# Expert outputs rounded and scattered in float32r, and three half chunks per expert left unsplit

## The chip, the cores and the metric

One core of one Trainium2 chip. The metric is the device time of the whole program in microseconds (us); the kernel before takes 2283.22 us, the median of three runs (2280.13 to 2283.72).

## The reference

256 tokens of width 2048, all in float32. A conformer block (causal convolution, feed-forward) is followed by a second block, whose last part is a hierarchical mixture of 16 experts; the change lies there. Each token goes to 2 of 16 experts; an expert is `silu(x @ w_gate) * (x @ w_up)` of width 512, times the token's gate, times `w_down` back to 2048, and the outputs are summed into the tokens:

```python
hid = silu(einsum('td,edf->tef', t, w_gate)) * einsum('td,edf->tef', t, w_up)
y = einsum('tef,efd->td', hid * gate[:, :, None], w_down)
```

The result passes through a final RMS norm.

## The kernel before

**The weight stream.** All large weights come through one class, `Stream`. Its order is a list of chunks of 128 x 2048 float32 (1 MB). `load` issues one DMA per chunk from SP's queue into one of four `raw` buffers. A chunk is used as two halves of 128 x 1024. Each half is split for exactness: `hi` is the half rounded to float32r (a copy on ScalarE, line 74), `lo` is the rest (a subtraction on VectorE, line 83). In the expert stage `hi` is issued up to four halves ahead of the half being multiplied and `lo` up to three (`MOE_HI`, `MOE_LO`); there are 5 `hi` and 4 `lo` buffers. When the second half's `lo` has been issued, the chunk's buffer is given to the load four chunks later. TensorE multiplies the other operand, itself kept as a high and a low part, with `hi` and with `lo` (`product`: two matmuls of 512 columns, both float32r).

**The expert stage.** An expert has 16 half chunks of gate and up weights and 8 of down weights. The order of the turns is in(0), in(1), out(0), in(2), out(1), in(3), and so on to in(14), out(13), out(14), in(15), out(15); "in" is `into`, "out" is `down`. An expert holds 64 token slots. `into(e)` makes four matmuls per half; its 128 output rows are the 64 slots' high parts and low parts. `between(e)` then copies the two result banks out (line 1163 scales gate by the token's norm), folds the two row halves with float32 matmuls, applies silu, multiplies, and splits the hidden layer into high and low. These seven steps are run one per half during the next out. `down(e)` makes four matmuls per half; each two halves complete 512 output columns in one bank, and ScalarE copies the bank to `Yt` (line 1203). There are three `Yt` buffers.

**Scatter.** `scatter(k, es)` multiplies a 128 x 128 piece of `Yt` with the float32 matrix `sc` of the expert (slot to token, holding gate and norm), 256 columns in float32, for a pair of experts (e-1, e) with e even, into a spare bank; VectorE then adds the bank to the tokens `h` (line 1148). The scatters wait in a list `todo` and are filled in behind the products by a credit: each half adds 0.5 (0.1 where the next group's tokens are gathered, 0.3 in the last in), and a scatter of two experts costs 0.86.

**Order.** Each engine runs its instructions in the order in which the program issues them. One `beat` per half issues: `hi` and `lo` of later halves, then what was posted at the half before (copies out of banks, adds), then one step of `between`; then come the products and the fill. Gathers of the next four experts' tokens are done in in(0) and during in(3), in(7) and in(11), two 512-column copies' worth of work on ScalarE and TensorE per half.

**Before the expert stage** the same `Stream` feeds three matmuls of 256 or 272 columns per weight block, from about 17 us to about 1650 us of the span. `y` is a constant buffer of 16 KB per partition.

Of the kernel before, what the change touches and what calls it, by code (L numbers as in the profile page):

```python
# [7 lines left out]
F32 = mybir.dt.float32  # L8
# [4 lines left out]
OP = mybir.AluOpType  # L13
# [24 lines left out]
    VOFF[_name] = NV  # L38
    NV += _n

RAW_BUFS, HI_BUFS, LO_BUFS = 4, 5, 4
FILL_GU, FILL_DOWN, FILL_GATHER = 0.5, 0.5, 0.1
FILL_LAST = 0.3
LEAD, TURN, LATE, ON_PE = 3, 15, 4, 27
# [4 lines left out]
class Stream:  # L49
# [3 lines left out]
    def __init__(self, nc, raw, parts, order):  # L53
        self.nc, self.raw, self.parts, self.order = nc, raw, parts, order
        self.ahead, self.limit = (HI_BUFS, LO_BUFS), 2 * len(order)
        self.loaded = self.n_high = self.n_low = self.pos = 0
        self.raws, self.highs, self.lows = {}, {}, {}

    def load(self, upto):
        while self.loaded < min(upto, len(self.order)):  # L60
            t = self.raw.tile([P, 2048], F32, tag="raw", name=f"raw{self.loaded}")
            self.nc.sync.dma_start(out=t, in_=self.order[self.loaded][0])
            self.raws[self.loaded] = t
            self.loaded += 1

    def source(self, half):
        i, s = divmod(half, 2)
        self.load(i + 1)
        return self.raws[i][:, s * 1024 : (s + 1) * 1024]

    def high_to(self, halves):
        while self.n_high < halves:
            hi = self.parts.tile([P, 1024], F32R, tag="hi", bufs=HI_BUFS, name=f"hi{self.n_high}")
            self.nc.scalar.copy(hi, self.source(self.n_high))  # L74
            self.highs[self.n_high] = hi
            self.n_high += 1

    def low_to(self, halves):
        while self.n_low < halves:
            i, s = divmod(self.n_low, 2)  # L80
            eng = self.nc.gpsimd if self.order[i][1] else self.nc.vector
            lo = self.parts.tile([P, 1024], F32R, tag="lo", bufs=LO_BUFS, name=f"lo{self.n_low}")
            eng.tensor_tensor(lo, self.source(self.n_low), self.highs[self.n_low].bitcast(F32), OP.subtract)  # L83
            self.lows[self.n_low] = lo
            self.n_low += 1
            if s == 1:
                del self.raws[i]
                self.load(i + 1 + RAW_BUFS)

    def split_to(self, half, back=0):  # L90
        self.high_to(min(half + self.ahead[0] - back, self.limit))
# [40 lines left out]
def network(ctx, tc, a, out):  # L132
# [62 lines left out]
    y = const.tile([P, KB, T], F32, name="y")  # L195
# [751 lines left out]
    for k in range(14, KB):  # L947
        router(k)
    rn3 = small([2], "rn3")
    lt = wE.tile([20, T], F32, name="lt")  # L950
    natural_sums(pr, 2, lone)
    nc.scalar.copy(lt, lp)
    nc.scalar.activation(rn3, pr[:, 0:4:2], ACT.Sqrt, bias=eps6)
# [119 lines left out]
        nc.vector.tensor_reduce(nmore, more, AX, OP.add)  # L1073
        nc.vector.tensor_copy(nmore_i, nmore)

    yx = wE.tile([P, 8, T], F32, name="yx")
    Yt = [t.rearrange("p a t -> p (a t)") for t in (y[:, :8, :], y[:, 8:, :], yx)]

    def experts(hot, stream, extra):
        scat, rsl, hids, left = {}, {}, {}, [0] * NE  # L1080


        jobs, todo, posts, credit, ring = deque(), deque(), deque(), [0.0], deque((6, 7))
# [42 lines left out]
        def spread(e):  # L1126

            b, o = spare()
            for n in range(2):
                mm(o[:, n * T : (n + 1) * T], idt[: 2 * NE, n * NE + e : n * NE + e + 1].to_broadcast([2 * NE, P]), placeT, n == 0, True)  # L1130
            sc = wF.tile([P, T], F32, tag="sc", bufs=5, name=f"sc{e}_{turn_of[0]}")
            rs = wF.tile([P, 1], F32, tag="rs", name=f"rs{e}_{turn_of[0]}")

            def scale():
                nc.vector.scalar_tensor_tensor(sc, o[:, :T], slot_col, rb, OP.is_equal, OP.mult, accum_out=rs)
                nc.vector.tensor_tensor(sc, o[:, T:], sc, OP.mult)

            post(scale, b)
            scat[e], rsl[e] = sc, rs

        def scatter(k, es):
            b, o = spare()
            for n, e in enumerate(es):
                mm(o[:, :T], Yt[e % 3][:, k * P : (k + 1) * P], scat[e], n == 0, n == len(es) - 1)
                left[e] -= 1

            def add():
                nc.vector.tensor_tensor(h[:, k, :], h[:, k, :], o[:, :T], OP.add)
                if NE - 1 in es:
                    post(square)  # L1150

            def square():
                sq = square_to(k)
                nc.scalar.activation(sq, h[:, k, :], ACT.Square)
                post(lambda: add_square(sq, k, True))

            post(add, b)

        def between(e):
            gu = wF.tile([P, 2, 512], F32, tag="gu", bufs=1, name=f"gu{e}_{turn_of[0]}")  # L1160

            def out_of_bank():
                nc.scalar.activation(gu[:, 0, :], bank[0], ACT.Copy, scale=rsl[e])
                nc.scalar.copy(gu[:, 1, :], bank[1])

            def folded(g):

                for f in range(4):
                    mm(bank[4 + g][:, f * P : (f + 1) * P], gu[:, g, f * P : (f + 1) * P], fold, f == 0, True)

            view = lambda g: bank[4 + g].rearrange("p (f s) -> p f s", f=4)[:, :, :CAP]
            sg = wF.tile([P, 4, CAP], F32, tag="sg", bufs=1, name=f"sg{e}_{turn_of[0]}")
            hd = wF.tile([P, 4, P], F32R, tag="hd", name=f"hd{e}_{turn_of[0]}")
            hids[e] = hd

            def silu():
                nc.scalar.activation(sg, view(0), ACT.Silu)

            def high():
                nc.scalar.copy(hd[:, :, :CAP], sg)  # L1180
                if e == NE - 1:
                    nc.scalar.preload_act_table(ACT.Sqrt)

            return deque([out_of_bank, lambda: folded(0), lambda: folded(1),
                    silu,
                    lambda: nc.vector.tensor_tensor(sg, view(1), sg, OP.mult),
                    high,
                    lambda: nc.vector.tensor_tensor(hd[:, :, CAP:], sg, hd[:, :, :CAP].bitcast(F32), OP.subtract)])

        def down(e):  # L1190
            while e >= 3 and left[e - 3] > 0:
                todo.popleft()[1]()
            hd = hids.pop(e)
            left[e] = KB
            for c in range(4):
                o = bank[2 + c % 2]
                for n in range(2):
                    hi, lo = beat()
                    for f in range(2):
                        product(o, hd[:, 2 * n + f, :], hi, lo, f, n == 0 and f == 0, n == 1 and f == 1)  # L1200
                    if n == 1:
                        def out_of_bank(c=c, o=o):
                            nc.scalar.copy(Yt[e % 3][:, c * 512 : (c + 1) * 512], o)

                            es = (e,) if e in (0, NE - 1) else (e - 1, e)
                            if e == NE - 1 or e % 2 == 0:
                                for k in range(4 * c, 4 * c + 4):
                                    todo.append((0.43 * len(es), lambda k=k: scatter(k, es)))
                        post(out_of_bank)
                    fill(FILL_DOWN if e < NE - 1 else 1)  # L1210

        def into(e):
            nxt = one_hot(e // 4 + 1) if e % 4 == 3 and e + 1 < NE else None
            for k in range(KB):
# [6 lines left out]
                for kk in ([k - 3] if e == 0 else [k]) if k < KB - 1 or e else range(KB - 4, KB):  # L1221
# [3 lines left out]
                    w = X(kk)[:, (e % 4) * P : (e % 4 + 1) * P]  # L1225
                    for g in range(2):
                        product(bank[g], w, hi, lo, g, kk == 0, kk == KB - 1)
                    if extra is not None:
                        next(extra, None)
                    if kk == 13:  # L1230
# [28 lines left out]
                posts.popleft()()  # L1259


        natural_sums(bank[2], 2, lone)
        rsqrt(rp, bank[2][:, :4:2], eps6)
        to_all(rp, bank[3][:, :T])
        for k in range(KB):
            nc.vector.scalar_tensor_tensor(y[:, k, :], h[:, k, :], V("final", k), bank[3][:, :T], OP.mult, OP.mult)  # L1266
            if k in (1, 3, 7, 11, 15):
                k0 = {1: 0, 3: 2}.get(k, k - 3)
                nc.sync.dma_start(out=out[:, k0 : k + 1, :], in_=y[:, k0 : k + 1, :])

    experts(hot, stream, gates())
    turn_of[0] = "more"
# [65 lines left out]
```

## Time and profile before

| | |
|---|---|
| median of 3 runs | 2283.22 us (2280.13 to 2283.72) |
| the profiled execution | 2283.07 us, of which the span is 2281.3 us |
| TensorE (PE) busy | 2219.8 us, 97% |
| VectorE (DVE) busy | 1596.8 us, 70% |
| ScalarE (ACT) busy | 1255.5 us, 55% |
| DMA loads of weights | 460 of 1 MB each |
| expert stage, first product to start of the last out | 1679.6 to 2243.9 us |

PE's busy time is modelled: matmuls overlap, so the distance between two starts is the cost of one, not its duration. In the rows, `hi`, `lo`, `raw`, `sc`, `hd`, `gu`, `y`/`yx` (the buffers of `Yt`) and `x` (the tokens `h`) are the program's tiles. A float32 matmul stands in two records.

### The profile page before, as it was taken

The page shows a single profiled execution, that of the slowest core. Times are in us where ns is not written, and L with a number is a line of the kernel's source. Part 1 is how long each engine was busy: PE and PEld are TensorE (multiplying, and loading weights), DVE is VectorE, ACT ScalarE, POOL GpSimd, SP SyncE. Part 2 cuts the span into 40 slices and gives each one's busy share as a digit, 9 for nine tenths or more (in the row PEclk, how much of TensorE's full clock was granted, in tenths as well). Part 3 has the DMA queues.
Part 4 walks back from the last instruction along what each step waited for, and adds up shares of the span by engine and source line. Part 5 has one row for each costly group of instructions (what it writes and reads, how often), then busy time and mean ns, then how long its engine had stood idle before and what let it go on. Part 6 is the DMA issues. An engine that isn't in the chain of part 4 may idle for free. (4 is left out here: it accounts for less than half of the span.)

```text
span 2281.3 us, 40365 instructions
## 1 busy us (share of the span) xinstructions
PE 2219.8 (97%) x16539; PEld 2079.1 (91%) x16539; DVE 1596.8 (70%) x2259; ACT 1255.5 (55%) x1638; POOL 214.6 (9%) x162
## 2 busy tenths in 40 slices
PE   6999999999999999999999999999999999999996
PEld 6999899999999999999899999999976878778785
DVE  7999767655544455555875664566579899888996
ACT  4445555544434444444553444444577878778774
POOL 5798100000000000001100000000000000000001
PEclk8999999999999999999999999999999999999998
DMA  5444354555555555555655555555559999999993
GB/s 212 167 166 161 101 202 167 187 200 188 200 188 200 189 198 191 191 198 188 222 185 196 193 185 188 198 190 201 169 205 367 355 351 355 331 348 344 354 357 135
DMA packets 71410, 508.79 MB, mean 223 GB/s; under 512 B 7936, under 2 KB 7952, under 8 KB 10288
## 3 DMA queue, kind: packets, MB, share of 16 engines
q1 hardware_dynamic: 70560, 503.85, 62.3%
q8 instruction: 131, 2.15, 0.4%
q0 software_dynamic: 656, 2.27, 0.3%
q14 instruction: 63, 0.52, 0.1%
HBM read 503.99 MB, written 2.10 MB: 222 GB/s over the span
## 5 line engine op out<-in xcount | busy, mean ns | idle before, releaser
L83 DVE TENSOR_TENSOR lo<-raw,hi 128x1024 fp32r<-128x1024 f32 x884 | 1064.1, 1222 | 534.4 <-PE bank L165 471.9
L74 ACT CAST hi<-raw 128x1024 fp32r<-128x1024 f32 x952 | 986.4, 1054 | 770.5 <-PE bank L165 674.6
L165 PE MATMUL bank<-aH,hi 128*128 128x256 f32 (+1 forms) x3456 | 965.4, 280 | 7.1 <-ACT aH L244 5.3
L165 PE MATMUL bank<-aL,hi 128*128 128x256 f32 (+1 forms) x3456 | 960.0, 279 | 8.0 <-DVE aL L246 8.0
L165 PE MATMUL bank<-aH,lo 128*128 128x256 f32 (+1 forms) x3456 | 962.6, 279 | 0.4 <-DVE lo L83 0.4
L165 PEld LDWEIGHTS bank<-aH,hi 128*128 128x128 f32 x3456 | 652.7, 189 | 10.1 <-ACT aH L244 5.7
L165 PEld LDWEIGHTS bank<-aL,hi 128*128 128x128 f32 x3456 | 649.8, 189 | 9.5 <-DVE aL L246 9.3
L165 PEld LDWEIGHTS bank<-aH,lo 128*128 128x128 f32 x3456 | 652.4, 189 | 0.6 <-DVE lo L83 0.6
L536 POOL TENSOR_TENSOR acc<-acc,sq 128x256 f32<-128x256 f32 x23 | 17.7, 768 | 1925.3 <-ACT sq L677 722.9
L165 PE MATMUL bank<-hidH,lo 128*128 128x256 f32 x704 | 194.3, 276 | 0.0
L165 PE MATMUL bank<-hidH,hi 128*128 128x256 f32 x704 | 194.3, 276 | 0.0
L165 PE MATMUL bank<-hidL,hi 128*128 128x256 f32 x704 | 194.3, 276 | 0.0
L83 POOL TENSOR_TENSOR lo<-raw,hi 128x1024 fp32r<-128x1024 f32 x68 | 163.4, 2415 | 52.8 <-ACT hi L74 33.1
L285 DVE SCALAR_TENSOR_TENSOR bank<-glu,vec,bank 128x256 f32<-128x256 f32 x387 | 160.6, 483 | 1.9
L165 PEld LDWEIGHTS bank<-hidH,hi 128*128 128x128 f32 x704 | 132.2, 188 | 0.0
L165 PEld LDWEIGHTS bank<-hidL,hi 128*128 128x128 f32 x704 | 132.2, 188 | 0.0
L165 PEld LDWEIGHTS bank<-hidH,lo 128*128 128x128 f32 x704 | 132.2, 188 | 0.0
L165 PE MATMUL bank<-hi,aH 128*128 128x512 f32 x320 | 128.8, 419 | 1.1 <-ACT hi L74 0.8
L165 PE MATMUL bank<-hi,aL 128*128 128x512 f32 x320 | 126.2, 411 | 0.0
L165 PE MATMUL bank<-lo,aH 128*128 128x512 f32 x320 | 123.3, 401 | 2.0 <-DVE lo L83 2.0
L165 PE MATMUL bank<-hi,hd_first 128*128 128x512 f32 x256 | 112.3, 439 | 0.1
L165 PE MATMUL bank<-lo,aL 128*128 128x512 f32 x256 | 103.3, 404 | 1.7 <-DVE lo L83 1.4
(284 smaller groups left out, 2181.9 us busy)
## 6 DMA issues: line engine op xcount, KB each, us to landing
raw<-egu SPq DMA_DIRECT2D x128, 1024.0 KB, 5.2
raw<-gu SPq DMA_DIRECT2D x88, 1024.0 KB, 4.8
raw<-w SPq DMA_DIRECT2D x72, 1024.0 KB, 4.8
raw<-edn SPq DMA_DIRECT2D x64, 1024.0 KB, 5.8
raw<-dn SPq DMA_DIRECT2D x44, 1024.0 KB, 4.8
raw<-cw_in SPq DMA_DIRECT2D x32, 1024.0 KB, 4.8
raw<-cw_out SPq DMA_DIRECT2D x16, 1024.0 KB, 4.8
raw<-wup SPq DMA_DIRECT2D x16, 1024.0 KB, 4.8
```

Source lines behind the costliest of these rows:

```text
L74: self.nc.scalar.copy(hi, self.source(self.n_high))
L83: eng.tensor_tensor(lo, self.source(self.n_low), self.highs[self.n_low].bitcast(F32), OP.subtract)
L165: nc.tensor.matmul(o, l, r, start=start, stop=stop, skip_group_check=True)
L285: nc.vector.scalar_tensor_tensor(dw[:, j, :] if t == end - 1 else ta, gl, V("w_dw", j * TAPS + t), early[j % 2] if t == 1 else ta, OP.mult ...
L536: (nc.gpsimd if n or gpsimd else nc.vector).tensor_tensor(acc[:, n, :], acc[:, n, :], sq, OP.add)
```

## The change

The expert stage is changed in three ways, and the stream in one.

1. Loads are of half a chunk (128 x 1024, 512 KB) into eight buffers of half the size, in the whole kernel. A buffer is given on after its own `lo`.
2. In the expert stage three half chunks of an expert are marked "whole": the second halves of chunks 2 and 5 of its gate and up weights (halves 5 and 11 of 16) and of chunk 1 of its down weights (half 3 of 8). They get no `hi` and no `lo`; the product takes the buffer itself in one float32 matmul in place of two float32r ones. Their buffer is kept until that product is done, and no load beyond the eighth half behind it is issued before (`done`).
3. `sc` becomes a 0/1 matrix in float32r and `Yt` is float32r. What the rounding loses is recovered: `lost` subtracts `Yt` from the bank by a matmul with minus the identity, and ScalarE copies 64 rows of what is left to `yl`. A scatter is then, per block, one float32r matmul per expert and one more with `yl` for the pair; it takes two blocks at once, with one add of 512 columns. The gate moves into the copy of the "up" bank (`gsl`). `Yt` has two buffers. `y` is no longer kept for the whole program; its space is taken by `Yt` and, at the end, by the output buffer.

```diff
-RAW_BUFS, HI_BUFS, LO_BUFS = 4, 5, 4
+RAW_BUFS, HI_BUFS, LO_BUFS = 8, 5, 4
     def load(self, upto):
-        while self.loaded < min(upto, len(self.order)):
-            t = self.raw.tile([P, 2048], F32, tag="raw", name=f"raw{self.loaded}")
-            self.nc.sync.dma_start(out=t, in_=self.order[self.loaded][0])
+        while self.loaded < min(upto, 2 * len(self.order), self.whole[0] + RAW_BUFS if self.whole else upto):
+            i, s = divmod(self.loaded, 2)
+            t = self.raw.tile([P, 1024], F32, tag="raw", name=f"raw{self.loaded}")
+            self.nc.sync.dma_start(out=t, in_=self.order[i][0][:, s * 1024 : (s + 1) * 1024])
+    def is_whole(self, half):
+        return self.order[half // 2][1] == "whole" and half % 2 == 1
+    def done(self):
+        if self.whole and self.whole[0] < self.pos:
+            del self.raws[self.whole.popleft()]
+            self.load(self.n_low + RAW_BUFS)
...
-        moe_order += [(a["egu"][e, c], False) for c in range(8)] if what == "in" else [(a["edn"][e, c], False) for c in range(4)]
+        moe_order += [(a["egu"][e, c], c in (2, 5) and "whole") for c in range(8)] if what == "in" else [(a["edn"][e, c], c == 1 and "whole") for c in range(4)]
...
         def product(o, x, hi, lo, g, first, last):
+            if hi is None:
+                mm(o, x.bitcast(F32), lo[:, sl], first, last)
+                return
...
+                nc.vector.scalar_tensor_tensor(scaled, o[:, :T], slot_col, rb, OP.is_equal, OP.mult, accum_out=rs)
+                nc.vector.scalar_tensor_tensor(scaled, scaled, 1.0, o[:, T:], OP.mult, OP.mult, accum_out=gs)
+                nc.vector.tensor_scalar(sc, o[:, :T], slot_col, None, OP.is_equal)
+                nc.scalar.copy(pairs[e][high_rows(e), :], sc[high_rows(e), :].bitcast(F32))
...
-                mm(o[:, :T], Yt[e % 3][:, k * P : (k + 1) * P], scat[e], n == 0, n == len(es) - 1)
+            for kk in (k, k + 1):
+                sl, to = slice(kk * P, (kk + 1) * P), o[:, kk % 2 * T : (kk % 2 + 1) * T]
+                for n, e in enumerate(es):
+                    mm(to, Yt[e % 2][:, sl], scat[e], kk == k and n == 0, False)
+                mm(to, yl[rows, sl], pairs[es[0]][rows, :], False, True)
...
-                nc.scalar.copy(gu[:, 1, :], bank[1])
+                nc.scalar.activation(gu[:, 1, :], bank[1], ACT.Copy, scale=gsl[e])
...
-            while e >= 3 and left[e - 3] > 0:
+            while e >= 2 and left[e - 2] > 0:
...
-                            nc.scalar.copy(Yt[e % 3][:, c * 512 : (c + 1) * 512], o)
+                        def out_of_bank(c=c, o=o, sl=sl):
+                            nc.scalar.copy(Yt[e % 2][:, sl], o)
+                            post(lambda: lost(c, o, sl))
+                        def lost(c, o, sl):
+                            mm(o, minus, Yt[e % 2][:, sl], False, True)
+                            nc.scalar.copy(yl[rows, sl], o[rows])
...
-                                    todo.append((0.43 * len(es), lambda k=k: scatter(k, es)))
+                                for k in (4 * c, 4 * c + 2):
+                                    todo.append((0.24 * (len(es) + 1), lambda k=k: scatter(k, es)))
```

## Rows read from the trace of the kernel before

**Rows 1.** First line of the profile's page.

```profile
span 2281.3 us, 40365 instructions
```

**Rows 2.** Stretches: us, busy time (instructions) by engine, TensorE clock, DMA share, GB/s.

```profile
400.00:700.00 300.00, 300.00 (x2648) 300.00 (x2647) 165.35 (x191) 138.52 (x177) 0.00 (x0) 1.00 0.57 194
...
1841.60:1861.70 20.10, 19.07 (x70) 11.60 (x69) 18.66 (x17) 16.05 (x17) 0.00 (x0) 1.00 0.99 406
1861.70:1877.40 15.70, 13.68 (x68) 11.25 (x67) 13.98 (x20) 13.25 (x18) 0.00 (x0) 1.00 0.90 336
1877.40:1901.10 23.70, 23.70 (x105) 19.42 (x104) 22.89 (x29) 16.75 (x19) 0.00 (x0) 1.00 0.97 360
1901.10:1912.30 11.20, 11.20 (x58) 9.51 (x57) 9.12 (x13) 8.80 (x14) 0.00 (x0) 1.00 0.85 292
1912.30:1936.80 24.50, 24.02 (x134) 20.16 (x133) 22.61 (x24) 24.35 (x34) 0.00 (x0) 1.00 0.98 380
1936.80:1950.80 14.00, 13.59 (x69) 11.28 (x69) 11.03 (x15) 12.09 (x18) 0.00 (x0) 1.00 0.84 297
...
1985.80:2007.40 21.60, 19.32 (x70) 11.58 (x68) 18.63 (x17) 16.02 (x17) 0.00 (x0) 1.00 0.98 374
2007.40:2024.70 17.30, 15.27 (x68) 12.64 (x67) 14.08 (x20) 13.45 (x18) 0.00 (x0) 0.90 0.86 312
...
2216.30:2243.90 27.60, 27.53 (x131) 22.69 (x129) 22.95 (x31) 19.39 (x23) 0.00 (x0) 1.00 0.77 303
2243.90:2258.20 14.30, 13.11 (x55) 10.07 (x56) 11.20 (x20) 9.34 (x18) 6.06 (x8) 1.00 0.01 2
```

**Rows 3.** TensorE's instructions in order: start, us, operation, shapes, count.

```profile
1906.09 0.39 PE L165 MATMUL bank<-lo,hd_first 128*128 128x512 f32 x1
1906.32 0.39 PE L165 MATMUL bank<-hi,hd_first 128*128 128x512 f32 x1
...
1906.78 1.03 PE L165 MATMUL bank<-sc_first,y 128*128 128x256 f32 x4
1907.46 0.58 PE L165 MATMUL bank<-hi,hd_first 128*128 128x512 f32 x1
1907.88 0.40 PE L165 MATMUL bank<-lo,hd_first 128*128 128x512 f32 x1
...
1915.82 0.40 PE L165 MATMUL bank<-hot_first,tL 128*128 128x256 f32 x2
1916.05 0.39 PE L165 MATMUL bank<-hi,aH 128*128 128x512 f32 x1
```

**Rows 4.** Groups of instructions, 1740 to 2281 us: count, busy us, mean ns, idle before.

```profile
L83 DVE TENSOR_TENSOR lo<-raw,hi 128x1024 fp32r<-128x1024 f32 x339 | 402.0, 1219 | 21.8 <-ACT hi L74 19.6 <-PE bank L165 1.4
L74 ACT CAST hi<-raw 128x1024 fp32r<-128x1024 f32 x337 | 346.0, 1057 | 69.6 <-PE bank L165 40.4 <-DMA raw<-egu 17.7 <-DMA raw<-edn 5.0
...
L1148 DVE TENSOR_TENSOR x<-x,bank 128x256 f32<-128x256 f32 x133 | 55.3, 419 | 31.3 <-PE bank L165 30.1
...
L1203 ACT COPY y<-bank 128x512 f32<-128x512 f32 x40 | 23.5, 587 | 14.6 <-PE bank L165 14.6
...
L1163 ACT ACTIVATE gu_first<-bank,rs_first 128x512 f32<-128x512 f32 x14 | 9.6, 684 | 6.0 <-PE bank L165 6.0
```

**Rows 5.** Instructions of an odd expert's out, in order of time.

```profile
1901.53 2.00 ACT L74 CAST hi<-raw 128x1024 fp32r<-128x1024 f32 x2
...
1908.78 0.59 ACT L1203 COPY yx<-bank 128x512 f32<-128x512 f32 x1 [0.99 <-PE bank L165]
```

**Rows 6.** Loads into raw, 1900 to 1930 us: time from issue to landing.

```profile
DMA to landing us min/median/max: 4.6/5.8/6.7
```

**Rows 7.** What SP's queue waited for, 1740 to 2230 us: total, times, longest.

```profile
SPq L62 <- DVE lo L83: 361.2, 144, 3.8
```

**Rows 8.** Stretches at the start (columns of Rows 2), rows of 2176 and 8192 bytes.

```profile
3.00:4.50 1.50, 0.00 (x0) 0.00 (x0) 0.15 (x1) 0.93 (x3) 0.00 (x0) 1.00 1.06 367
...
9.00:12.00 3.00, 2.83 (x8) 1.51 (x7) 1.68 (x4) 1.24 (x4) 0.00 (x0) 1.00 1.04 432
```

More of the change, by code (lines that the diff above doesn't have):

```diff
@@ L57, in __init__ @@
         self.raws, self.highs, self.lows = {}, {}, {}
+        self.whole = deque()
     def load(self, upto):
-        while self.loaded < min(upto, len(self.order)):
-            t = self.raw.tile([P, 2048], F32, tag="raw", name=f"raw{self.loaded}")
-            self.nc.sync.dma_start(out=t, in_=self.order[self.loaded][0])
+        while self.loaded < min(upto, 2 * len(self.order), self.whole[0] + RAW_BUFS if self.whole else upto):
+            i, s = divmod(self.loaded, 2)
+            t = self.raw.tile([P, 1024], F32, tag="raw", name=f"raw{self.loaded}")
+            self.nc.sync.dma_start(out=t, in_=self.order[i][0][:, s * 1024 : (s + 1) * 1024])
             self.raws[self.loaded] = t
@@ L66, in source @@
     def source(self, half):
-        i, s = divmod(half, 2)
-        self.load(i + 1)
-        return self.raws[i][:, s * 1024 : (s + 1) * 1024]
+        self.load(half + 1)
+        return self.raws[half]
+    def is_whole(self, half):
[4 more added lines that the diff above has]
+            self.load(self.n_low + RAW_BUFS)
     def high_to(self, halves):
         while self.n_high < halves:
+            if self.is_whole(self.n_high):
+                self.highs[self.n_high] = None
+                self.n_high += 1
+                continue
             hi = self.parts.tile([P, 1024], F32R, tag="hi", bufs=HI_BUFS, name=f"hi{self.n_high}")
@@ L79, in low_to @@
         while self.n_low < halves:
-            i, s = divmod(self.n_low, 2)
-            eng = self.nc.gpsimd if self.order[i][1] else self.nc.vector
+            if self.is_whole(self.n_low):
+                self.lows[self.n_low] = self.source(self.n_low)
+                self.whole.append(self.n_low)
+                self.n_low += 1
+                continue
+            eng = self.nc.gpsimd if self.order[self.n_low // 2][1] is True else self.nc.vector
             lo = self.parts.tile([P, 1024], F32R, tag="lo", bufs=LO_BUFS, name=f"lo{self.n_low}")
@@ L84, in low_to @@
             self.lows[self.n_low] = lo
+            del self.raws[self.n_low]
             self.n_low += 1
-            if s == 1:
-                del self.raws[i]
-                self.load(i + 1 + RAW_BUFS)
+            self.load(self.n_low + RAW_BUFS)
     def split_to(self, half, back=0):
@@ L194, in network @@
     aL = const.tile([P, KB, N0], F32R, name="aL")
-    y = const.tile([P, KB, T], F32, name="y")
+    ctxY = ctx.enter_context(ExitStack())
+    y = pool("wY", c=ctxY, side="right").tile([P, KB, T], F32, name="y")
     acc = const.tile([P, 2, T], F32, name="acc")
@@ L949, in network @@
     rn3 = small([2], "rn3")
-    lt = wE.tile([20, T], F32, name="lt")
+    lt = tw.tile([P, T], F32, tag="t", name="lt")[:20, :]
     natural_sums(pr, 2, lone)
@@ L1074, in gates @@
         nc.vector.tensor_copy(nmore_i, nmore)
-    yx = wE.tile([P, 8, T], F32, name="yx")
-    Yt = [t.rearrange("p a t -> p (a t)") for t in (y[:, :8, :], y[:, 8:, :], yx)]
+    yl = wE.tile([P, 8 * T], F32R, name="yl")
+    high_rows = lambda e: slice(e % 2 * CAP, (e % 2 + 1) * CAP)
+    minus = wE.tile([P, P], F32R, name="minus")
+    nc.scalar.activation(minus, idt, ACT.Copy, scale=-1.0)
+    ctxY.close()
     def experts(hot, stream, extra):
-        scat, rsl, hids, left = {}, {}, {}, [0] * NE
+        ctxZ = ExitStack()
+        wZ = pool("wZ", c=ctxZ, side="right")
+        Yt = [wZ.tile([P, 8 * T], F32R, name=f"Yt{n}_{turn_of[0]}") for n in range(2)]
+        scat, rsl, gsl, hids, left, pairs = {}, {}, {}, {}, [0] * NE, {}
         jobs, todo, posts, credit, ring = deque(), deque(), deque(), [0.0], deque((6, 7))
@@ L1130, in spread @@
                 mm(o[:, n * T : (n + 1) * T], idt[: 2 * NE, n * NE + e : n * NE + e + 1].to_broadcast([2 * NE, P]), placeT, n == 0, True)
-            sc = wF.tile([P, T], F32, tag="sc", bufs=5, name=f"sc{e}_{turn_of[0]}")
-            rs = wF.tile([P, 1], F32, tag="rs", name=f"rs{e}_{turn_of[0]}")
+            sc = wF.tile([P, T], F32R, tag="sc", bufs=3, name=f"sc{e}_{turn_of[0]}")
+            scaled = tw.tile([P, T], F32, tag="t", name=f"scaled{e}_{turn_of[0]}")
+            rs, gs = (wF.tile([P, 1], F32, tag=n, name=f"{n}{e}_{turn_of[0]}") for n in ("rs", "gs"))
@@ L1134, in scale @@
+            pairs[e] = pairs[e - 1] if e and e % 2 == 0 else wF.tile([P, T], F32R, tag="both", name=f"both{e}_{turn_of[0]}")
             def scale():
-                nc.vector.scalar_tensor_tensor(sc, o[:, :T], slot_col, rb, OP.is_equal, OP.mult, accum_out=rs)
-                nc.vector.tensor_tensor(sc, o[:, T:], sc, OP.mult)
+                nc.vector.scalar_tensor_tensor(scaled, o[:, :T], slot_col, rb, OP.is_equal, OP.mult, accum_out=rs)
+                nc.vector.scalar_tensor_tensor(scaled, scaled, 1.0, o[:, T:], OP.mult, OP.mult, accum_out=gs)
+                nc.vector.tensor_scalar(sc, o[:, :T], slot_col, None, OP.is_equal)
+                nc.scalar.copy(pairs[e][high_rows(e), :], sc[high_rows(e), :].bitcast(F32))
@@ L1138, in spread @@
             post(scale, b)
-            scat[e], rsl[e] = sc, rs
+            scat[e], rsl[e], gsl[e] = sc, rs, gs
         def scatter(k, es):
             b, o = spare()
-            for n, e in enumerate(es):
-                mm(o[:, :T], Yt[e % 3][:, k * P : (k + 1) * P], scat[e], n == 0, n == len(es) - 1)
-                left[e] -= 1
+            rows = slice(0, P) if len(es) == 2 else high_rows(es[0])
+            for kk in (k, k + 1):
[3 more added lines that the diff above has]
+                mm(to, yl[rows, sl], pairs[es[0]][rows, :], False, True)
@@ L1147, in add @@
+            for e in es:
+                left[e] -= 2
             def add():
-                nc.vector.tensor_tensor(h[:, k, :], h[:, k, :], o[:, :T], OP.add)
+                two = h[:, k : k + 2, :]
+                nc.vector.tensor_tensor(two, two, o.rearrange("p (a t) -> p a t", a=2), OP.add)
                 if NE - 1 in es:
[L1150 to L1155, printed above, removed]
+                    for kk in (k, k + 1):
+                        post(lambda kk=kk: square(kk))
@@ L1157, in scatter, with square @@
+            def square(kk):
+                sq = square_to(kk)
+                nc.scalar.activation(sq, h[:, kk, :], ACT.Square)
+                post(lambda: add_square(sq, kk, True))
             post(add, b)
@@ L1177, in silu @@
                 nc.scalar.activation(sg, view(0), ACT.Silu)
+            first, second = (slice(n * CAP, (n + 1) * CAP) for n in (e % 2, 1 - e % 2))
             def high():
-                nc.scalar.copy(hd[:, :, :CAP], sg)
+                nc.scalar.copy(hd[:, :, first], sg)
                 if e == NE - 1:
@@ L1187, in between @@
                     high,
-                    lambda: nc.vector.tensor_tensor(hd[:, :, CAP:], sg, hd[:, :, :CAP].bitcast(F32), OP.subtract)])
+                    lambda: nc.vector.tensor_tensor(hd[:, :, second], sg, hd[:, :, first].bitcast(F32), OP.subtract)])
         def down(e):
-            while e >= 3 and left[e - 3] > 0:
+            while e >= 2 and left[e - 2] > 0:
                 todo.popleft()[1]()
@@ L1200, in down @@
                         product(o, hd[:, 2 * n + f, :], hi, lo, f, n == 0 and f == 0, n == 1 and f == 1)
+                    stream.done()
                     if n == 1:
-                        def out_of_bank(c=c, o=o):
-                            nc.scalar.copy(Yt[e % 3][:, c * 512 : (c + 1) * 512], o)
+                        sl, rows = slice(c * 512, (c + 1) * 512), high_rows(e)
+                        def out_of_bank(c=c, o=o, sl=sl):
[4 more added lines that the diff above has]
+                            nc.scalar.copy(yl[rows, sl], o[rows])
                             es = (e,) if e in (0, NE - 1) else (e - 1, e)
                             if e == NE - 1 or e % 2 == 0:
-                                for k in range(4 * c, 4 * c + 4):
-                                    todo.append((0.43 * len(es), lambda k=k: scatter(k, es)))
+                                for k in (4 * c, 4 * c + 2):
+                                    todo.append((0.24 * (len(es) + 1), lambda k=k: scatter(k, es)))
                         post(out_of_bank)
@@ L1227, in into @@
                         product(bank[g], w, hi, lo, g, kk == 0, kk == KB - 1)
+                    stream.done()
                     if extra is not None:
@@ L1259, in experts @@
                 posts.popleft()()
+        ctxZ.close()
+        ctxO = ExitStack()
+        last = pool("wO", c=ctxO, side="right").tile([P, KB, T], F32, name=f"last_{turn_of[0]}")
         natural_sums(bank[2], 2, lone)
@@ L1265, in experts @@
         for k in range(KB):
-            nc.vector.scalar_tensor_tensor(y[:, k, :], h[:, k, :], V("final", k), bank[3][:, :T], OP.mult, OP.mult)
+            nc.vector.scalar_tensor_tensor(last[:, k, :], h[:, k, :], V("final", k), bank[3][:, :T], OP.mult, OP.mult)
             if k in (1, 3, 7, 11, 15):
                 k0 = {1: 0, 3: 2}.get(k, k - 3)
-                nc.sync.dma_start(out=out[:, k0 : k + 1, :], in_=y[:, k0 : k + 1, :])
+                nc.sync.dma_start(out=out[:, k0 : k + 1, :], in_=last[:, k0 : k + 1, :])
+        ctxO.close()
     experts(hot, stream, gates())
```

## The prediction

> **What bounds the kernel now.** I read the page first: the profiled execution took 2283.07 us around a span of 2281.3 us [rows 1], 0.15 us below the median of 2283.22, so sums against it need no correction. Then the stretches. In the dense stages TensorE never stops (300 us busy of 300) while the DMA engines are at 0.57 [rows 2]; smaller loads have room there, and I cost them at nothing. All else lies in the expert stage, so I cut it at the changes between in and out and read which resource fills each block [rows 2].
> - In of an even expert (1877.40:1901.10, 23.7 us; six alike): TensorE busy all 23.70 us. Products: 64 at 0.23 us (1906.09 to 1906.32 [rows 3]), 14.7 us. A scatter of two experts: 0.68 us to the next start, and that start's successor 0.19 late, 0.87 us, 0.435 us per float32 matmul of 256 columns [rows 3]. Nine of them make 7.8 us; a spread of like size makes 23.4.
> - Out of an odd expert (1901.10:1912.30, 11.2 us; seven): TensorE full, ScalarE 8.80 us and waiting for TensorE's banks [rows 2, 5].
> - In of an odd expert: with gathers 24.5 us (1912.30:1936.80; three), ScalarE busy 24.35. Without (1841.60:1861.70, 20.1 us, and the slowest 1985.80:2007.40, 21.6; three in all), the DMA at 0.98 to 0.99 and up to 406 GB/s [rows 2].
> - Out of an even expert: 14.0 us behind a gather, 15.7 or 17.3 behind a block without [rows 2]. There ScalarE, whose queue is in order, stood at copies that waited for loads, with the hidden layer's steps behind them.
> So four resources take turns, each near its limit. Totals over the stage say little; the change must be costed block by block.
>
> **The parts, by engine.**
> *Whole halves* (48). Four float32r matmuls go, 0.92 us; two float32 ones of 512 columns come. No such row exists. A float32 matmul stands in two records; if each were as cheap as a float32r one (0.23), the product would cost 0.46 and the half nothing more. By columns the 256-wide float32 row gives 2 x 0.435 = 0.87, and four float32r passes 0.92. I take 0.87, of the same type: +0.82 us a half, +39 us of TensorE. ScalarE loses 48 copies of 1.06 us (1.00 back to back [rows 4, 5]), VectorE 48 subtractions of 1.22 [rows 4]: about -48 and -58.
> *Scatter in float32r.* 256 float32 matmuls at 0.435 go (111 us). Seven pairs x 16 blocks x 3 and two single experts x 16 x 2 are 400 float32r matmuls of 256 columns at 0.115 (two from 1915.82 to 1916.05 [rows 3]): 46 us. `lost` adds 64 at 0.23: 15. TensorE in all: 39 - 111 + 46 + 15 = -11 us of some 560. VectorE: 144 adds of 0.42 [rows 4] become 72 of twice the width, between 0.42 and 0.84; I take 0.69, as the 1024-wide subtraction at 1.22 shows that width is cheaper than count. That is -10, against +8 for a third operation per spread. ScalarE gains 64 copies of `yl` at 0.59 [rows 4] and 16 of half the columns, by estimate 0.4: +44, net about -4. So VectorE is freed, TensorE slightly, ScalarE hardly, and DMA bytes stay.
>
> **Block by block.** A scatter item is now 6 x 0.115 = 0.69 us of TensorE and 0.72 of credit; of a pair's eight, five fall into the out that makes them and three into the following in.
> - *Even in, six*: TensorE 14 x 0.92 + 1.74 x 2 + 0.87 (spread) + 3 x 0.69 = 19.3. VectorE 22.89 less two subtractions (2.4) and nine adds (3.8), plus three wide adds and 0.5: 19.3. Loads: 16 x 0.524 MB at 406 GB/s = 20.7. The DMA is next. I take 20.7: -3.0 each, -18.
> - *Odd out, seven*: TensorE stays at 11.2 (two scatters go, 1.74; whole half and `lost` come, 1.74). But here a wait is added. `lost` stands in TensorE's queue and waits for the copy to `Yt`; that copy stands in ScalarE's queue behind a `hi` copy; behind `lost` wait all later products; and the product two halves on waits for `yl` to leave the bank. I walked one out through, from its start, with 1.0 per `hi`, 0.6 per `Yt` or `yl` copy, 0.68 per gate copy [rows 4, 5], 0.2 from a matmul's end to its reader, and 0.9 per fold (products and two scatters leave 2.1 of the 11.2 for two). ScalarE: two gate copies to 1.3, two `hi` to 3.3, `Yt`(0) to 3.9, `hi` to 4.9, `yl`(0) (after `lost`(0) at 4.8) to 5.5, silu 5.85, `hi` 6.85, `Yt`(1) 7.4, `hi` 8.4, `yl`(1) 8.95, a hidden copy 9.3, `hi` 10.25, `Yt`(2) 10.8. TensorE: three products and both folds to 4.6, `lost`(0) 4.8, the whole half to 6.6, a product and `lost`(1) to 7.7, a product to 8.7, then waits for `yl`(1) until 9.0, product to 9.9, waits for `Yt`(2), product to 12.0. One more wait of 0.7 falls into the next in (`lost`(3)). 12.7 for 11.2: +1.5 each, +10.5. Ends: 0 if ScalarE were always free, +3.1 if its whole sum (7 x 1.06 + 8 x 0.6 + 2.1 = 14.3) must pass within the block.
> - *Odd in with gathers, three*: ScalarE loses two `hi`, gains about 1.5; TensorE is 14 x 0.92 + 3.5 + 16 x 0.46 + 0.87 + 0.23 = 24.8. +0.3 each, +1.
> - *Odd in without*: TensorE 17.5, VectorE 18.63 - 2.4 + 0.5 = 16.7; loads 20.7 less the lead won in the longer out before (12.7 against 10.3 for its loads). I take 18.8: -1.3, -2.8, -1.3.
> - *Even out*: TensorE 7 x 0.92 + 1.74 + 1.9 (folds) + 0.92 (`lost`) + 5 x 0.69 = 14.4, long enough for ScalarE's copies. Behind gathers +0.4 three times; behind the others 15.1, a part of the old stall stays: -0.6, -2.2, -0.6.
> - *Last in, out and tail* (27.6 and 14.3 us [rows 2]): scatters no longer fill the chain between them, -1.5; cheaper scatters in the last out, -1.0; at the very end `lost` and `yl` stand between `Yt` and the last scatters, +1.3.
> The first turns, in(0) to in(3) but for out(1), I leave at zero. Sum: -18 + 10.5 + 1 - 5.4 + 1.2 - 3.4 - 1.2 = -15.3, which gives 2268.
>
> **Loads.** *Rows of 4096 bytes.* The nearest rows: 432 GB/s with 8192-byte rows, 367 with 2176 [rows 8]. So 406 becomes between 345 and 406; I take 406, as a 4096-byte row is nearer in kind to a long one. At 345 an even in takes 24.3. *The kept buffer.* Loads stop at eight halves behind a whole half until its product is done; today SP mostly waits for `lo` [rows 7], three halves earlier. Eight halves move in 8 x 1.29 = 10.3 us, and a load needs about 3.3 to land (the shortest of 4.6 for 1 MB [rows 6], less the 1.29 of the half that is gone). So the queue runs dry only if a whole half landed more than 7 us before its product ends. Then TensorE has as much in store, and the pause eats store, not time, while the DMA has slack elsewhere (the outs, 11 to 14 us for 10.3 of loads).
> A 1 MB load lands 5.8 us after its issue [rows 6]. The Trainium skill (DMA: Bandwidth & Descriptors, Anatomy of one DMA) gives each DMA a fixed cost of about 2.0 us plus its bytes at 436 GB/s and calls 860 KB the half-efficient size; by that 512 KB are worse than 1 MB, and if loads went singly 384 of 3.2 us would be 1230 us instead of 564. The trace speaks against it: at 406 GB/s and 5.8 us more than two loads are under way at once. I give it 1 in 100.
>
> **Rivals.**
> 1. *ScalarE's queue decides the outs (slower).* Odd outs at the upper end, 14.3 (+22 in place of +10.5), even outs 2 us longer behind gathers (+6), gather blocks +1 (+3): -15 + 11 + 9 = +5, 2288. For it: ScalarE is at 24.35 of 24.5 in a gather block and waits behind loads in others. Against: 8.80 of 11.2 in the odd out. It turns the sign once the odd outs reach 15, or 14 with the even outs.
> 2. *The loads decide (slower).* At 345 GB/s two experts need 25.2 MB, 73 us, as long as now (23.7 + 11.2 + 24.5 + 14.0); with the pauses 2 to 3 us per pair more, 2300.
> 3. *The waits stay hidden.* Odd outs 11.2 and even ins at TensorE's 19.3: -15.3 - 10.5 - 8 = -34, 2249.
> 4. *Balance without gain*: what one block wins the next gives back as in the even outs today: 2283.
>
> **Chances.** Forecast (2261 to 2277) 0.45; rival 3 0.18; rival 1 0.20; rival 2 with the skill's 0.08; rival 4 0.09. The range 2248 to 2293 leaves out the loads' case and the far end of rival 3. This kernel's runs tell 0.2% (4.6 us) from no change: faster 0.63, same 0.13, slower 0.24, with the low half of rival 1 in same.
>
> **What would show it.** Right: even ins near 20.7 us at full DMA share, odd outs near 12 to 13 with TensorE waiting for ScalarE's `Yt` and `yl`, two records of about 0.43 us apiece per whole product, fewer waits for loads. Wrong: odd outs at 14 or more; the float32 product far from 0.87; DMA share full below 380 GB/s; or a dense stage that moved.

## The result and the profile after

The changed kernel takes 2299.43 us (median of 4, 2298.1 to 2302.33) against 2281.68 us for the kernel before (now a median of 4): ratio 1.0072, 95% interval 1.0056 to 1.0088. It is slower by 0.7%, where 2268 and a gain were forecast; the range (2248 to 2293) misses it. The profiled execution took 2299.42 us; its span is 16.4 us longer than the one before [rows 1]. One execution among all those below, one of v1_odd_tail, took 4470 us, about twice the others, and is left out of its median and ratio.

First line of the page of the changed kernel:

```profile
span 2297.7 us, 41419 instructions
```

Stretches of the changed kernel, columns as in [rows 2] (the engines are TensorE, its weight loads, VectorE, ScalarE and GpSimd):

```profile
400.00:700.00 300.00, 300.00 (x2649) 300.00 (x2648) 165.47 (x192) 138.83 (x178) 0.00 (x0) 1.00 0.61 195
...
1853.00:1871.90 18.90, 18.00 (x70) 12.72 (x69) 14.82 (x13) 14.17 (x16) 0.00 (x0) 1.00 0.98 363
1871.90:1890.60 18.70, 16.16 (x82) 12.97 (x82) 14.38 (x21) 14.44 (x21) 0.00 (x0) 0.91 0.93 344
1890.60:1910.50 19.90, 19.90 (x89) 14.94 (x88) 18.94 (x23) 13.58 (x17) 0.00 (x0) 1.00 0.95 332
1910.50:1923.50 13.00, 11.60 (x52) 8.06 (x52) 10.58 (x13) 12.55 (x19) 0.00 (x0) 1.00 1.02 402
1923.50:1949.70 26.20, 25.78 (x135) 20.39 (x134) 18.32 (x20) 22.55 (x33) 0.00 (x0) 1.00 0.94 338
1949.70:1964.80 15.10, 14.49 (x83) 11.79 (x82) 11.59 (x14) 13.46 (x21) 0.00 (x0) 1.00 0.86 298
...
2253.50:2272.40 18.90, 18.27 (x60) 12.17 (x61) 8.94 (x10) 10.51 (x19) 4.87 (x7) 0.91 0.01 1
```

Against [rows 2], in this order: a dense stretch (unchanged), an in without gathers (18.9 for 20.1), the even out behind it (18.7 for 15.7), an even in (19.9 for 23.7, TensorE still full), an odd out (13.0 for 11.2, ScalarE at 12.55, TensorE no longer full), an in with gathers (26.2 for 24.5), the even out behind it (15.1 for 14.0). The last row is most of the last out, which with the tail behind it runs from 2253.5 to the end, 44.2 us for 37.4. All blocks, cut at the first product of each:

| blocks | predicted, sum | measured, sum |
|---|---|---|
| 6 even ins | -18 | -23.0 |
| 5 odd outs (3 to 11) | +7.5 | +11.6 |
| out 1 | +1.5 | +6.3 |
| 3 ins with gathers | +1 | +2.6 |
| 3 ins without | -5.4 | -4.3 |
| 3 even outs behind gathers | +1.2 | +3.3 |
| 3 even outs behind the others | -3.4 | +4.4 |
| in 0, in 1, out 0, in 2 | 0 | +6.2 |
| out 13 and out 14 | +1.5 | +3.7 |
| last in | -1.5 | -1.3 |
| last out and tail | +0.3 | +6.8 |
| all | -15.3 | +16.3 |

The even ins came out better than forecast and the other ins within 2 us of it; the outs and the two ends did not. Of the first turns' +6.2, 1.1 lie ahead of the first product of in 0. Two places that the prediction had not looked at show in the trace. The first, where an even out begins (start, us, engine; in brackets the idle time before and its releaser):

```profile
1873.61 0.40 ACT L1172 CAST both_first<-sc_first 64x256 fp32r<-64x256 f32 x1 [1.32 <-DVE sc_first L1171]
1874.04 1.04 ACT L89 CAST hi<-raw 128x1024 fp32r<-128x1024 f32 x1
1875.11 0.69 ACT L1207 ACTIVATE gu_first<-bank,rs_first 128x512 f32<-128x512 f32 x1
1875.69 0.68 ACT L1208 ACTIVATE gu_first<-bank,gs_first 128x512 f32<-128x512 f32 x1
1875.85 2.07 PE L184 MATMUL bank<-fold,gu_first 128*128 128x128 f32 x8 [2.51 <-ACT gu_first L1207]
```

The small copy of the 0/1 rows into the pair's matrix stands in ScalarE's queue ahead of a `hi` copy and the two gate copies. It waits 1.32 us for VectorE's new third operation of the spread, which stands behind VectorE's subtractions, which wait for ScalarE's `hi`. Fold and all products behind it wait 2.51 us. TensorE's clock fell after that wait: granted 0.50, the lower of its levels, in the first row below, and 0.58 on average in the second, behind the 3.66 us that TensorE waited ahead of the last out.

```profile
1875.80:1878.20 2.40, 2.35 (x10) 2.26 (x11) 1.40 (x2) 2.40 (x3) 0.00 (x0) 0.50 1.03 420
...
2253.50:2257.40 3.90, 3.90 (x11) 3.05 (x12) 2.93 (x3) 3.10 (x5) 0.00 (x0) 0.58 0.00 0
```

Who waited for whom in the expert stage and the tail (total, times, longest), before:

```profile
ACT hi L74 <- DMA raw<-egu: 17.9, 24, 2.5
...
PE bank L165 <- ACT gu_first L1163: 8.9, 9, 2.0
...
ACT hi L74 <- DMA raw<-edn: 6.5, 10, 1.3
```

In the changed kernel:

```profile
ACT hi L89 <- DMA raw<-egu: 26.0, 34, 3.8
ACT both_first L1172 <- DVE sc_first L1171: 25.4, 16, 4.6
PE bank L184 <- ACT gu_first L1207: 20.2, 16, 2.5
...
PE bank L184 <- ACT Yt_first L1252: 10.6, 15, 0.9
...
ACT hi L89 <- DMA raw<-edn: 6.5, 17, 1.2
```

TensorE's wait for the gate copies more than doubled, the wait for the small copy is new, and ScalarE's waits for loads rose from 24.4 to 32.5 us.

The second place is TensorE's own work. Its instructions in order: a single expert's scatter, a whole half, a pair's scatter.

```profile
1734.24 0.28 PE L184 MATMUL bank<-sc_first,Yt_first 128*128 128x256 f32 x1
1734.45 0.38 PE L184 MATMUL bank<-both_first,yl 64*128 64x256 f32 x1
1734.77 0.39 PE L184 MATMUL bank<-sc_first,Yt_first 128*128 128x256 f32 x1
...
1748.73 1.88 PE L184 MATMUL bank<-raw,aH 128*128 128x512 f32 x4
1750.04 0.80 PE L184 MATMUL bank<-hi,aH 128*128 128x512 f32 x1
1750.68 0.40 PE L184 MATMUL bank<-lo,aH 128*128 128x512 f32 x1
...
1886.39 0.40 PE L184 MATMUL bank<-sc_first,Yt_first 128*128 128x256 f32 x2
1886.62 0.28 PE L184 MATMUL bank<-both_first,yl 128*128 128x256 f32 x1
1886.74 0.40 PE L184 MATMUL bank<-sc_first,Yt_first 128*128 128x256 f32 x2
```

A pair's three matmuls take 0.35 us (1886.39 to 1886.74), 0.12 each, as costed. The whole half takes 1750.68 - 1748.73 less one float32r matmul's 0.23: 1.72 for the 1.74 forecast. But a single expert's second matmul has 64 rows, and where 64 and 128 rows alternate each, of either shape, costs 0.31 (1734.45 to 1734.77) in place of 0.115. The two single experts' scatters have 64 matmuls, 32 of each shape: 12.5 us more in all.

### The profile page after: what moved, and what is told of

It is laid out like the page before. It is cut to its first block, busy times and chain, and to the rows that moved or that the text cites. A ratio compares the mean times of both kernels' runs of the same rounds, so it can differ in the third digit from the quotient of the medians.

```text
span 2297.7 us, 41419 instructions
## 1 busy us (share of the span) xinstructions
PE 2221.4 (97%) x16491; PEld 2053.9 (89%) x16491; DVE 1549.4 (67%) x2171; ACT 1254.6 (55%) x1671; POOL 214.1 (9%) x162
## 5 line engine op out<-in xcount | busy, mean ns | idle before, releaser
L102 DVE TENSOR_TENSOR lo<-raw,hi 128x1024 fp32r<-128x1024 f32 x836 | 1011.8, 1223 | 596.9 <-PE bank L184 469.9
L89 ACT CAST hi<-raw 128x1024 fp32r<-128x1024 f32 x904 | 940.0, 1053 | 757.7 <-PE bank L184 570.5
L184 PE MATMUL bank<-hi,aL 128*128 128x512 f32 x288 | 113.8, 413 | 0.0
L184 PE MATMUL bank<-hi,aH 128*128 128x512 f32 x288 | 113.2, 411 | 0.2 <-ACT aH L582 0.2
L184 PE MATMUL bank<-lo,aH 128*128 128x512 f32 x288 | 107.7, 392 | 0.0
L184 PE MATMUL bank<-hi,hd_first 128*128 128x512 f32 x224 | 97.1, 433 | 4.7 <-DVE hd_first L1234 3.7
L184 PE MATMUL bank<-lo,hd_first 128*128 128x512 f32 x224 | 90.5, 404 | 0.0
```

## The experiments

Each was compared with the kernel before on the same chip (2282.2 or 2283.2 us there); the changed kernel was not run beside them. The edits are to the changed kernel unless said.

**e1_rows128**: the single experts' second matmul with 128 rows.

```diff
+    nc.gpsimd.memset(yl.bitcast(F32), 0.0)
...
+            if e in (0, NE - 1):
+                nc.gpsimd.memset(pairs[e][high_rows(e + 1), :].bitcast(F32), 0.0)
...
-            rows = slice(0, P) if len(es) == 2 else high_rows(es[0])
+            rows = slice(0, P)
```

> The two single experts' second scatter product takes 128 rows in place of 64 (the other 64 rows of its 0/1 matrix are zero). Theory 64 rows: in the changed kernel the 128 matmuls of the two single experts' scatters stand 0.31 us apart where the pairs' stand 0.12, so that the out of expert 0, the in behind it and the last out lose 128 x 0.19 = 24 us of TensorE, of which about half is on the path (the last out and the out of expert 0): 12 us faster, about 2287. Rival (ScalarE's waits set these blocks): under 3 us, the matmuls get close but the blocks keep their length.

Measured 2296.59 us, 1.0058 (1.0046 to 1.0070): about 3 us less than the changed kernel, with intervals that overlap. The theory counted 128 matmuls; there are 64, so it should have said 12 us of TensorE and 6 on the path. The matmuls do close up to 0.12 (TensorE in order):

```profile
2263.00 0.28 PE L184 MATMUL bank<-sc_first,Yt_first 128*128 128x256 f32 x1
2263.12 0.28 PE L184 MATMUL bank<-both_first,yl 128*128 128x256 f32 x1
2263.24 0.28 PE L184 MATMUL bank<-sc_first,Yt_first 128*128 128x256 f32 x1
```

The cost is real, the blocks keep most of their length: out 0 is 1.7 us shorter, the last out 2.4, where TensorE now waits 2.0 us at once for `Yt`. Neither number fitted; the rival was nearer.

**e2_copy_late**: the small copy goes with the second fold, behind the gate copies.

```diff
-                nc.scalar.copy(pairs[e][high_rows(e), :], sc[high_rows(e), :].bitcast(F32))
...
+            def one_of_pair():
+                folded(1)
+                nc.scalar.copy(pairs[e][high_rows(e), :], scat[e][high_rows(e), :].bitcast(F32))
...
-            return deque([out_of_bank, lambda: folded(0), lambda: folded(1),
+            return deque([out_of_bank, lambda: folded(0), one_of_pair,
```

> The small copy of the 0/1 rows into the pair's matrix is issued three halves later, behind the two gate copies. Theory copy in the way: ScalarE stood 25 us in all in front of it (16 times, for VectorE), and the gate copies, the folds and the later products stood behind it, with a slow clock after the longest waits: 10 to 15 us faster, about 2287, the outs behind a block without gathers back to 16 us or less, the odd outs to 12.5. Rival (the loads are late there anyway, ScalarE then waits for them instead): under 4 us, and the waits for loads grow by what this wait loses.

Measured 2283.41 us, 1.0009 (0.9999 to 1.0019): by moving 16 copies, 16 us of the 17.7 lost are gone by the medians, 14 of 16 by the ratios. The out that took 18.7 us takes 15.6, at full clock, and the gate copies keep TensorE 4.8 us in place of 20.2. Half of the gain, 8.2 us, lies in the three outs behind ins without gathers, which are now 3.8 us shorter in all than before, near the 3.4 forecast. The odd outs stay at 13.0, not 12.5. The rival saw little: ScalarE's waits for loads rose only from 32.5 to 37.6 us. This kernel's stretch and wait:

```profile
1866.30:1881.90 15.60, 14.65 (x82) 11.74 (x81) 14.16 (x21) 14.35 (x21) 0.00 (x0) 1.00 1.01 402
```
```profile
PE bank L184 <- ACT gu_first L1206: 4.8, 10, 1.0
```

**c1_both**: both edits. 

> Both edits at once. If the two causes are separate and complete, 2299 - 12 - 12 = 2275, faster than the kernel before. If the loads or ScalarE's sum decide, 2287 or more.

Measured 2278.31 us, 0.9980 (0.9970 to 0.9989): with the copy out of the way the 128 rows bring 5 us more. The sum of 2275 is nearly met, but not by its parts: 16 and 3 to 5, for 12 and 12.

**e4_no_whole**: nothing is marked whole (`False` for both marks).

> No half is kept whole: all are split, no buffer is held; loads of half a chunk and the float32r scatter stay. By the prediction's costs TensorE loses 39 us of work, ScalarE gains 48 us and VectorE 58: the outs and gather blocks, full on ScalarE, grow by 1 each, the even ins fall back to VectorE's 21.7: about 2310, slower than the changed kernel. Rival (the kept buffers stop the loads and cost more than the split they save): 2285 or less, with fewer waits of ScalarE for loads.

Measured 2317.97 us, 1.0156 (1.0143 to 1.0170). The direction is the theory's, the size is not the split alone: the same two waits grew (small copy 31.0 us, gate copies to TensorE 37.7), so this kernel can't price whole halves by itself.

```profile
PE bank L184 <- ACT gu_first L1207: 37.7, 16, 3.2
ACT both_first L1172 <- DVE sc_first L1171: 31.0, 16, 4.2
```

**b1_half_loads**: the kernel before, with only the loads halved (`RAW_BUFS` 8, tiles of 1024 columns).

> The kernel before with one part of the change alone: loads of half a chunk into eight half buffers. The changed kernel's dense stages kept their length (300 us busy of 300) and its DMA share only rose from 0.57 to 0.61, so nothing there. In the expert stage the even ins ran without a stall at 4096-byte rows. Theory loads harmless: 2282, within 3 us. Rival (smaller rows move less, the blocks bound by loads grow): the ins without gathers 21 us or more, 2290.

Measured 2275.58 us, 0.9969 (0.9958 to 0.9980): a gain that neither theory had. Its gain lies where loads were waited for: ScalarE's waits for them fall from 24.4 us to 11.0 (rows below), in 0 and in 1 are 1.5 us shorter, in 3 2.1, in 9 2.1, the out behind it 1.6. The loads did not land sooner after their issue (median 6.2 us from 1680 to 2230 us, 5.4 before), which speaks for their earlier issue as the cause; it was not tested apart.

```profile
ACT hi L74 <- DMA raw<-egu: 7.3, 28, 0.7
...
ACT hi L74 <- DMA raw<-edn: 3.7, 18, 0.4
```

**w1_whole_only**: the kernel before with half loads and whole halves, scatter in float32.

> The kernel before with half loads and whole halves, scatter in float32 as before. TensorE gets 39 us more work and nothing back; ScalarE and VectorE get 48 and 58 us less. Theory block by block: even ins 25.3 (+1.6), odd outs 12, ins with gathers 24.8, ins without 19, outs behind them 15: about +12, 2294. Rival (the kept buffer's pause in the loads is the main loss): ins without gathers over 20 and waits of ScalarE for loads above 40 us in all, 2305 or more.

Measured 2293.74 us, 1.0051 (1.0036 to 1.0066), the theory's number, with some luck: the theory counted no gain from half loads, and against b1_half_loads whole halves cost 18 us, not 12. An even out behind an in without gathers, an even in and an odd out of this kernel (columns as in [rows 2]):

```profile
1861.60:1876.60 15.00, 14.44 (x69) 11.35 (x68) 12.93 (x18) 12.54 (x17) 0.00 (x0) 1.00 1.01 396
1876.60:1901.90 25.30, 25.30 (x106) 19.43 (x105) 20.56 (x27) 14.37 (x16) 0.00 (x0) 1.00 0.97 340
1901.90:1913.90 12.00, 12.00 (x59) 9.53 (x58) 8.62 (x12) 8.47 (x13) 0.00 (x0) 1.00 0.82 271
```

15, 25.3 and 12 were forecast; the ins with gathers took 25.7 on average for 24.8. TensorE's sum sets the even ins and odd outs. The held buffers can at most show in expert 9's in (20.8 us for 19.4 in b1_half_loads), though ScalarE's waits for loads (35 us) are three times those of b1_half_loads.

**c2_both_dve**: c1_both with `yl` copied by VectorE (`nc.vector.tensor_copy(yl[rows, sl], o[rows])`).

> Both mended places, and the copy of what the rounding lost (yl, 64 copies of 0.58 us) done by VectorE in place of ScalarE. Theory ScalarE's queue holds up the outs: odd outs fall from 13 to 12 or less, the last out by 2 us, 8 to 10 us below c1_both (2278): 2269. Rival (VectorE's own queue, with the subtractions in front of the copy, holds the bank as long): no gain or a loss of up to 5 us, TensorE then waits for yl in the place of Yt.

Measured 2279.95 us, 0.9990 (0.9979 to 1.0001): no gain over c1_both. Odd outs fall to 12.3 on average (13.2 in c1_both) and the last out and its tail by 2.8, but even outs, where VectorE also adds the scatters, rise by 1.1 to 2.1. The wait has moved as the rival said, from the first line (c1_both) to the second (this kernel):

```profile
PE bank L184 <- ACT Yt_first L1258: 16.1, 23, 2.0
```
```profile
PE bank L184 <- DVE yl L1264: 12.4, 19, 1.1
```

**c3_mended_no_whole**: c1_both without whole halves. 

> Both mended places, no whole halves. The unmended kernel lost 19 us without whole halves. If whole halves are worth the split work that they spare, the same here: 2297. If they were worth it only because the small copy stood in the way, 2285 or less.

Measured 2275.69 us, 0.9967 (0.9957 to 0.9978): the second case. With c1_both at 0.9980 the two can hardly be told apart.

**v1_odd_tail, v2_fewer_whole, v3_none_whole**: c1_both with each block's better choice.

```diff
-FILL_LAST = 0.3
+FILL_LAST = 0.0
...
-                            nc.scalar.copy(yl[rows, sl], o[rows])
+                            (nc.vector.tensor_copy if e % 2 else nc.scalar.copy)(yl[rows, sl], o[rows])
...
-                    fill(FILL_DOWN if e < NE - 1 else 1)
+                    fill(1 if e == NE - 1 else 0 if e == NE - 2 else FILL_DOWN)
```

v2 also has `and e % 4 != 3` and `and e % 4 != 2` in the marks of the in and out chunks, which unmarks the last in too; v3 marks none.

> Both mended places; yl copied by VectorE for odd experts and by ScalarE for even ones; the last pair's scatters are held back to the chain between the last in and the last out. By the blocks of c1_both and c2_both_dve: odd outs 0.8 less seven times, the last out 3 less, the chain filled so that TensorE's clock does not fall, 3: 2278 - 11 = 2267. Rival (the outs move into the next block): 2275 or more.

> As v1, without whole halves in the three ins with gathers and the outs behind them (and the out of expert 14), where c3_mended_no_whole's blocks were 0.8 us shorter each: 2262. Rival (those blocks' copies come from the stretch before them): no better than v1.

> As v1, without any whole half: 2276 (c3_mended_no_whole) - 11 = 2265, if whole halves are worth nothing once the waits are mended; above 2270 if ScalarE and VectorE, with the split of 48 more halves, hold the outs behind ins without gathers (17 to 18 us there against 15).

Measured: v1 2267.39 us (median of 5), 0.9940 (0.9925 to 0.9955); v2 2259.83 us, 0.9898 (0.9883 to 0.9913; four runs); v3 2268.52 us, 0.9946 (0.9928 to 0.9964). The first two met their numbers, v3 lies between its two cases. In v1 odd outs 3 to 11 take 11.7 us on average, outs 13 and 14 24.1 together (27.2 in c1_both), the last out and tail 2.9 less. v2 beats both kernels, the one before by 1.0%; against v1 the ins with gathers and the outs behind them are 7.3 us shorter in all, as expected. An odd out, an in with gathers and the out behind it, in v2:

```profile
1894.80:1907.00 12.20, 11.26 (x52) 8.07 (x51) 11.80 (x15) 11.75 (x17) 0.00 (x0) 1.00 1.03 418
1907.00:1932.00 25.00, 24.39 (x135) 20.32 (x134) 23.71 (x27) 23.34 (x33) 0.00 (x0) 1.00 0.96 358
1932.00:1946.00 14.00, 13.63 (x83) 11.76 (x82) 11.77 (x15) 13.56 (x21) 0.00 (x0) 1.00 0.91 333
```

The medians in one table, all with half loads (the kernel before had 2281.7 to 2283.2 beside them):

| scatter | no half whole | three whole |
|---|---|---|
| float32, as before | 2275.6 | 2293.7 |
| float32r, as changed | 2318.0 | 2299.4 |
| float32r, copy late, 128 rows | 2275.7 | 2278.3 |
| the same, `yl` by parity, last fill held back | 2268.5 | 2267.4 |

Half loads alone bring 7 us. Whole halves cost 18 us beside the float32 scatter, where TensorE is short; they save 19 beside the float32r scatter as changed, where ScalarE and VectorE are short; and, marked in every expert, are worth nothing once those waits are mended. Kept out of the blocks that v2 names and marked in the rest, they bring 8 us over marking all or none. The float32r scatter as changed costs 42 us without whole halves and 6 with them; mended it costs nothing, or brings 15. No part has a price of its own.

## Why the prediction was wrong

**The step that failed** is the scatter part's ScalarE term: "16 of half the columns, by estimate 0.4". The copy's duration was right (0.40), its place was not asked for; the sum gave it 6 us of ScalarE's work and no wait. It waits for VectorE (25.4 us in all), in a queue in which the gate copies stand behind it. The prediction did this walk for `lost` and `yl` in the outs and left this copy out of it, so the walk of an odd out began with the gate copies at 0 us. In the odd outs 3 to 11 the first now starts 0.8 to 1.7 us after the out's first product, 0.7 ahead of it before. Expert 5's out, which begins at 1901.14 before and at 1910.54 after:

```profile
1900.48 0.68 ACT L1163 ACTIVATE gu_first<-bank,rs_first 128x512 f32<-128x512 f32 x1
```
```profile
1910.10 0.41 ACT L1172 CAST both_first<-sc_first 64x256 fp32r<-64x256 f32 x1 [1.34 <-DVE sc_first L1171]
1910.41 1.05 ACT L89 CAST hi<-raw 128x1024 fp32r<-128x1024 f32 x1
1911.36 0.67 ACT L1207 ACTIVATE gu_first<-bank,rs_first 128x512 f32<-128x512 f32 x1
```

In the even out shown above it starts 3.2 us after the out (2.5 before). The even outs behind ins without gathers, forecast shorter by 3.4 us in all, became longer by 4.4. e2_copy_late shows the copy to be 14 to 16 us of the loss.

**The 64-row matmuls** are the second: 400 matmuls were costed at 0.115 from rows of 128-row ones, and no bound was set for the other shape. Once the copy is out of the way, 128 rows bring 5 us: the first turns are 4.6 us shorter and the last out 2.4 (c1_both against e2_copy_late), 7 of the 13 us that these two lost. Of the 4.2 left in the last out, 2.8 go with `yl` on VectorE (c2_both_dve). The Trainium skill (TensorE: Matmul & The Clock Gate, Why this matters for your kernels) says that a single matmul of 32 rows takes as long as one of 128. No run here has 64-row matmuls by themselves; alternated with 128-row ones, 64-row ones took 0.31 us for 0.12, and the 128-row ones between them as long.

**The first turns at zero** were a choice not worked out: +6.2. Out 1, forecast at +1.5, took +6.3. It is 10.0 us in w1_whole_only, so it is the scatter's waits there too, not the held buffers: 14.5 in c1_both, 11.8 in c2_both_dve, where ScalarE is rid of `yl`.

**What is left.** With both mended (c1_both) the profiled span is 6.4 us shorter than before, for the 15.3 forecast. Odd outs with out 1 took +14.3 for +9.0, the last out +4.2 for +0.3, the ins with gathers and the outs behind them +5.1 for +2.2; the even ins gave 23.0 for 18.

**What held.** The whole product at 0.87 (1.72 per half measured). TensorE's terms for the even ins (19.3 worked out, 19.9 measured, TensorE full); the load bound of 20.7 taken there was too careful. The odd outs' walk: 12.0 + 0.7 forecast; 13.2 on average in c1_both, where the copy no longer disturbs it. The ins without gathers took 18.9 for 18.8.

**The rivals and signs.** Rival 1's mechanism, ScalarE's queue with 2288 as its price, was the nearest, by another instruction of that queue than it named. Rival 2's number, 2300, was met by chance: e2_copy_late has the same loads and held buffers and took 2283. From 1740 to 2200 us the loads moved 343 GB/s at a DMA share of 0.94, 350 at 0.94 before: 2% less at the same share, where the lower bound of 345 for 406 was 15%. The sign "DMA share full below 380 GB/s" came up in the ins without gathers (363 at 0.98 in the row above), but it was there before as well (374 at 0.98 [rows 2]), and these ins became shorter. Fewer waits for loads, a sign of being right, did not come: 32.5 us for 24.4. The held buffers' pause ate store rather than time, as far as w1_whole_only shows. By the size rule of the Trainium skill (DMA: Bandwidth & Descriptors, Anatomy of one DMA), a fit for loads issued from GpSimd, 512 KB should be worse than 1 MB. Half loads alone, issued from SP's queue, were better (0.9969); that a buffer goes back after 512 KB is the likely reason.

**Open.** v1 changes two things at once; how its 11 us over c1_both divide between `yl` by parity and the held-back scatters was not measured alone, nor was the price of the lower clock, which the waits bring with them.

## What to carry to other kernels

Cost an added instruction first by what it waits for and who stands behind it in its queue, and only then by its duration: 16 copies of 0.4 us made 14 to 16 us here. When four resources are each near their limit block by block, price a part in the company it will keep; the same whole halves cost 18 us, saved 19 or did nothing. A matmul of another shape needs its own row or a bound.

## What the runs showed of the hardware

Alternating matmuls of 64 and 128 rows, 256 columns, float32r: 0.31 us apart, against 0.12 with 128 rows throughout (e1_rows128). A float32 matmul of 512 columns: 0.86 us, 3.7 times the 0.23 of float32r. After TensorE had waited 2.5 and 3.7 us, its granted clock was 0.50 over 2.4 us and 0.58 over 3.9 us. Loads with rows of 4096 bytes moved 402 GB/s (e2_copy_late) and 418 (v2_fewer_whole) over an out, with rows of 8192 bytes 406 over an in before; over 460 us of the expert stage it was 343 and 350 GB/s, both at a DMA share of 0.94.
